# Down projection by half-size matrix products: first-half products of all pairs ahead, next operands prepared in mid-chunk

## The chip, the cores and the metric

One core of one Trainium2 chip. The time is the device time of one execution in microseconds (us), lower is better; the kernel before has a median of 1379.69 us over 3 runs.

## The reference, cut to what matters

One layer of a decoder trunk over 1024 tokens with 1024 channels, all in f32. The part that matters here is the channel mixer and what follows it:

```python
h = rmsnorm(x, g_ffn[i])
u = jnp.einsum("bsd,df->bsf", h, w_up[i])                 # 1024 -> 2 x 2816
f_gate = causal_dwconv(u[..., :D_FF], conv_f_w[i]) + conv_f_b[i]
f = jax.nn.gelu(f_gate, approximate=True) * u[..., D_FF:]
x = x + jnp.einsum("bsf,fd->bsd", f, w_down[i])           # 2816 -> 1024, the stage that is changed
pg = jax.nn.sigmoid(jnp.einsum("bsd,de->bse", rmsnorm(x, g_ple[i]), w_ple_gate[i]))
x = x + pg * jnp.einsum("bsk,kd->bsd", p[i], w_ple[i])
```

## The kernel before

**Layout.** Channels lie on the 128 partitions, tokens on the free axis. A tile ("slot") is 128 x 1024 f32; 54 slots (`NBIG`) hold everything, weights in flight too. `H0` and `H1` are the first and second 512 tokens. A matmul multiplies a 128 x 128 weight block by 128 x 512 activations into one of 8 PSUM banks. To keep f32 accuracy every operand is split: `halve` writes hi (a rounding copy on ACT, L132) and lo (a subtraction on DVE, L133), and a block product is three matmuls, hi*hi, hi*lo and lo*hi (L629).

**Seven products instead of eight.** A 2 x 2 block product (two output row tiles, two token halves, two input row tiles) is made by a Strassen-like scheme, class `Pair`: product 1 and 2 use the plain halves, products 3 to 7 use sums of weight blocks and (3 excepted, on the activation side) sums of activation halves. Products 1 and 2 accumulate in bank `a`, a copy of product 1 goes to bank `b` (ACT, L639) and products 6, 7 and 4 are added to it; products 5 and 3 accumulate in bank `c`. In between, `b` is copied to `e` after 6 and after 7 (ACT, L646 and L652). After 2, `use11` takes `a`; when 5 and 7 are both made, `sum(22)` reads `c` and `e`; after 4, `use21` takes `b`; after 3, `sum(12)` reads `c` and `e`. Product 3 is accumulated in the bank that `sum(22)` has to have read. In the up projection that read is L665.

**The down projection.** `f`, the 22 row tiles of the up projection's result, is stored to DRAM (`f_d`) and read back in three chunks of 4, 4 and 3 rows (`DROWS`); row i of a chunk is a pair of tiles, `f_d[k]` and `f_d[11 + k]`. For each chunk four output pairs (tiles j and j + 4) make their seven products, 3n matmuls each for n rows. The results of the first two chunks go through `dn` tiles to `x1_d` in DRAM by an accumulating DMA on POOL (L1152, class `DnStore`); the last chunk adds them to `x1`, loaded back, in SBUF (class `DnLast`, L1173) and makes the scaled halves `xp` and the square sums for the last stage.

**Operands of a chunk.** Class `Rows`: `load` fetches the two tiles of a row (512 KB each); `plain` splits the first halves for products 1 and 2 (`f_q`); `sums` makes four half-width sums (L586 to L589, `t13` and `t24`), splits both sums tiles (`fs`, `ft`) and the half of product 3 (`f_q`). `prepare` calls them by how many products are left before the chunk: loads at 14 (chunk 0: at 6 and 3), plain at 5 (chunk 0: 5 and 3), sums of row 0 at 2, of row 1 at 1, of rows 2 and 3 at 0.

**Weights.** Class `Loader` issues weight loads on SP in the order of their use, each a fixed number of matmuls ahead (`AHEAD`: r, for products 1 and 2, 110; q, for product 4, 100; s, the sums for products 3, 5, 6 and 7, 150) and as far as slots are free. The sums of an s weight are made by four accumulating DMAs on POOL, in a chain (L243, L244). A weight is split 40 matmuls ahead of its use.

**Order.** PE and SP run in the order of the program text. ACT, DVE and POOL are ordered by a scheduler that takes what it thinks is ready, earliest in the text first, with its own costs; on the chip each engine then works strictly in that order. `block_order(4, 2)` gives the order of products in a chunk; m is the product's number and p the pair:

```python
# block_order(4, 2): (p, m)
# (0,1) (1,1) (0,2) (1,2) (0,6) (0,5) (0,7) (0,4) (1,6) (0,3) (1,5) (1,7)
# (2,1) (1,4) (2,6) (2,2) (1,3) (2,5) (2,7)
# (3,1) (2,4) (3,6) (3,2) (2,3) (3,7) (3,5) (3,4) (3,3)
```

The up projection has 22 pairs in the same scheme with 12 matmuls a product and ends with (21,7), (21,5), (21,4), (21,3). After each of its last products `f_rows.prepare(0, left)` is called.

Of the kernel before, what the change touches and what calls it, by code (L numbers as in the profile page):

```python
# [8 lines left out]
F32R = mybir.dt.float32r  # L9
# [20 lines left out]
HB = 512  # L30
# [44 lines left out]
def trunk_kernel(ctx, tc, xT, pT, par, w_in, w_a, w_b, w_o, w_up, w_dn, w_ple, w_pg, outT):  # L75
# [54 lines left out]
    def halve(hi, lo, src):  # L130

        nc.scalar.copy(hi, src)  # L132
        nc.vector.tensor_sub(lo, src, f32(hi))  # L133
# [191 lines left out]

    def in_tiles(kind, i):
# [25 lines left out]
    dn_order = block_order(KD // 2, 2)  # L352
    for ci, (k0, n) in enumerate(DROWS):
        ld.add_pairs(("dn", ci), [(w_dn[j], w_dn[KD // 2 + j]) for j in range(KD // 2)], dn_order, k0, KH + k0, n)
# [4 lines left out]
    with tc.manual_schedule(engines={PE, SP}):  # L359
# [241 lines left out]
        def half_split(src, name):  # L601

            t = slot(name, F32R)
            halve(t[:, :HB], t[:, HB:], src)
            return t[:, :HB], t[:, HB:]
# [482 lines left out]
        class Rows:  # L1088


            def __init__(self):
                self.rows = [[{} for _ in range(n)] for _, n in DROWS]
                self.raw = {}

            def load(self, ci, i):
                k = DROWS[ci][0] + i
                self.raw[ci, i] = load(f_d[k], "f"), load(f_d[KH + k], "f")

            def plain(self, ci, i):
                a, b = self.raw[ci, i]  # L1100
                r = self.rows[ci][i]
                r[1], r[2] = half_split(a[:, H0], "f_q"), half_split(b[:, H0], "f_q")

            def sums(self, ci, i):
                a, b = self.raw[ci, i]
                r = self.rows[ci][i]
                r.update(sum_halves(*right_sums(a[:, H0], a[:, H1], b[:, H0], b[:, H1]), "f"))
                r[3] = half_split(b[:, H1], "f_q")

            def prepare(self, ci, left):  # L1110

                n = DROWS[ci][1]
                if left == (6 if ci == 0 else 14):
                    for i in range(2 if ci == 0 else n):
                        self.load(ci, i)
                if left == 5:
                    for i in range(2 if ci == 0 else n):
                        self.plain(ci, i)
                if left == 3 and ci == 0:
                    for i in range(2, n):  # L1120
                        self.load(ci, i)
                        self.plain(ci, i)
                if left == 2:
                    self.sums(ci, 0)
                if left == 1:
                    self.sums(ci, 1)
                if left == 0:
                    for i in range(2, n):
# [313 lines left out]
```

## Time and profile before

| | us |
|---|---|
| median of 3 runs (1376.6 to 1381.29) | 1379.69 |
| the profiled execution, as timed | 1382.37 |
| its span, first to last instruction | 1380.6 |
| TensorE busy in the span | 1306.8 |
| mean granted TensorE clock, share of full | 0.972 |

Times within the trace are microseconds from the start of the span. A row of a timeline is an instruction (or several alike, x2) with its start, its duration and, in brackets, how long its engine had been idle and what ended that. Matmuls are pipelined, so one has a duration of 0.39 us although the next begins 0.23 us later; pace is read from starts. A view by stretch gives each engine's busy time within a stretch, the mean granted TensorE clock, the mean busy share of the 16 DMA engines and what they moved. SPq and POOLq are the queues on which DMAs are issued.

### The profile page before, as it was taken

Reading aid. Unit: us, or ns where it says so; the run is one execution under the profiler, and the core shown is the slowest. Engines: PE = TensorE matmul, PEld = TensorE weight load, DVE = VectorE, ACT = ScalarE, POOL = GpSimd, SP = SyncE. Lnnn points to the kernel's source line nnn. Section 1 sums busy time; section 2 is a strip of 40 time slices with the busy share of each in tenths; the row PEclk is TensorE's granted clock in tenths of the full one; section 3 lists DMA queues with packets and bytes.
Section 4 is the critical chain, followed back from the end, with each engine's and each line's share of the span. In section 5 each row is a group of like instructions: output and inputs, shape, how many; then the busy total and the mean of one; then the engine's idle time right before and its main releaser. Section 6 shows DMA issues by size and latency. Waiting matters only on the chain.

```text
span 1380.6 us, 15699 instructions
## 1 busy us (share of the span) xinstructions
PE 1306.8 (95%) x5798; PEld 1081.9 (78%) x5798; DVE 976.6 (71%) x1134; ACT 590.3 (43%) x814; POOL 247.1 (18%) x319
## 2 busy tenths in 40 slices
PE   9989999999999999899999999999976979989996
PEld 7768888788887788778888888888864867867996
DVE  7969999999448766486665566665676292588787
ACT  7443233233444334354344433444344262456554
POOL 1331221122100001122221222212112222320011
PEclk9989999999999999999999999999998999999998
DMA  9645696578676303597666776667666998994222
GB/s 339 183 119 125 179 237 159 142 200 212 196 272 233 122 24 130 163 205 189 177 167 175 198 186 172 174 168 192 187 181 162 272 222 204 211 234 153 76 91 73
DMA packets 102765, 245.25 MB, mean 178 GB/s; under 512 B 11680, under 2 KB 21664, under 8 KB 102688
## 3 DMA queue, kind: packets, MB, share of 16 engines
q1 hardware_dynamic: 61632, 148.81, 32.6%
q0 software_dynamic: 41056, 95.44, 32.1%
q8 instruction: 45, 0.74, 0.2%
q14 instruction: 32, 0.26, 0.1%
HBM read 173.42 MB, written 45.09 MB: 158 GB/s over the span
## 4 chain that ended last, share of the span: by engine, by line
PE 71%; DVE 14%; issue 8%; DMA 3%; ACT 2%; POOL 1%; SPq 0%; DVEq 0%; ACTq 0%; POOLq 0%
PE ps L629 50%; PE ps L155 14%; DVE acc L712 2%; PE ps L969 2%; PE ps L968 2%; PE ps L970 2%; DMA x_d<-dn 2%; DVE w_s_lo L133 1%; POOL s L244 1%; DMA f<-f_d 1%; DVE w_r_lo L133 1%; DVE x_raw L477 1%; DVE ft_lo L133 1%; DVE sc_cv L712 1%; DVE t L588 1%
## 5 line engine op out<-in xcount | busy, mean ns | idle before, releaser
L712 DVE SCALAR_TENSOR_TENSOR acc<-a,prm,acc 128x1023 f32<-128x1023 f32 (+14 forms) x120 | 151.8, 1265 | 1.7
L133 DVE TENSOR_TENSOR w_s_lo<-s,w_s_hi 128x1024 fp32r<-128x1024 f32 (+1 forms) x100 | 119.6, 1198 | 35.7 <-ACT w_s_hi L132 35.7
L244 POOL DMA_DIRECT2D s<-s x100 | 85.6, 856 | 298.2 <-DMA s<-s 126.0
L652 ACT COPY u<-ps 128x512 f32<-128x512 f32 x50 | 29.3, 586 | 202.3 <-PE ps L629 202.3
L132 ACT CAST w_s_hi<-s 128x1024 fp32r<-128x1024 f32 (+1 forms) x100 | 102.9, 1031 | 2.6 <-issue 1.7
L712 DVE SCALAR_TENSOR_TENSOR fg<-u_t,neg_f,fg 128x1023 f32<-128x1023 f32 (+1 forms) x44 | 56.5, 1283 | 28.3 <-ACT fg L706 27.6
L133 DVE TENSOR_TENSOR w_r_lo<-raw_r,w_r_hi 128x1024 fp32r<-128x1024 f32 (+1 forms) x50 | 59.8, 1197 | 17.2 <-ACT w_r_hi L132 17.2
L646 ACT COPY u<-ps 128x512 f32<-128x512 f32 x50 | 29.3, 586 | 92.4 <-PE ps L629 92.4
L629 PE MATMUL ps<-xgs_hi,w_s_lo 128*128 128x512 f32 x176 | 68.6, 390 | 0.0
L629 PE MATMUL ps<-xgs_lo,w_s_hi 128*128 128x512 f32 x176 | 68.5, 389 | 0.0
L629 PE MATMUL ps<-xgs_hi,w_s_hi 128*128 128x512 f32 x176 | 68.5, 389 | 0.0
L629 PE MATMUL ps<-xgp_hi,w_r_lo 128*128 128x512 f32 x176 | 68.5, 389 | 0.0
L629 PE MATMUL ps<-xgp_lo,w_r_hi 128*128 128x512 f32 x176 | 68.5, 389 | 0.0
L629 PE MATMUL ps<-xgp_hi,w_r_hi 128*128 128x512 f32 x176 | 68.5, 389 | 0.0
L639 ACT COPY ps<-ps 128x512 f32<-128x512 f32 x50 | 28.5, 571 | 87.6 <-PE ps L629 87.6
L1075 DVE TENSOR_TENSOR u_t<-ps,rstd 128x512 f32<-128x512 f32 x22 | 15.2, 691 | 69.7 <-PE ps L629 69.7
L155 PE MATMUL ps<-xp_hi,whi 128*128 128x448 f32 (+2 forms) x192 | 62.0, 323 | 1.9 <-DVE x L1201 1.9
L629 PE MATMUL ps<-xgq,w_s_hi 128*128 128x512 f32 x176 | 55.8, 399 | 7.2 <-DVE u_t L665 7.2
L155 PE MATMUL ps<-xp_lo,whi 128*128 128x448 f32 (+2 forms) x192 | 61.9, 323 | 0.0
L155 PE MATMUL ps<-xp_hi,wlo 128*128 128x448 f32 (+2 forms) x192 | 61.9, 323 | 0.0
L629 PE MATMUL ps<-xgt_hi,w_q 128*128 128x512 f32 x176 | 57.9, 390 | 0.7 <-ACT u L652 0.7
L629 PE MATMUL ps<-hss_hi,w_s_hi 128*128 128x512 f32 x128 | 50.9, 398 | 4.5 <-ACT w_s_hi L132 4.5
(297 smaller groups left out, 3718.7 us busy)
## 6 DMA issues: line engine op xcount, KB each, us to landing
s<-s POOLq DMA_DIRECT2D x92, 256.0 KB, 4.1
raw_r<-w_up SPq DMA_DIRECT2D x22, 512.0 KB, 4.7
s<-w_up SPq DMA_DIRECT2D x44, 256.0 KB, 3.0
s<-w_up SPq DMA_DIRECT2D x22, 512.0 KB, 5.8
s<-w_up POOLq DMA_DIRECT2D x44, 256.0 KB, 6.0
f_d<-v_t POOLq DMA_DIRECT2D x22, 512.0 KB, 5.9
f<-f_d SPq DMA_DIRECT2D x22, 512.0 KB, 9.8
s<-w_in SPq DMA_DIRECT2D x32, 256.0 KB, 3.2
```

The lines of the kernel that those rows point to most:

```text
L132: nc.scalar.copy(hi, src)
L133: nc.vector.tensor_sub(lo, src, f32(hi))
L155: nc.tensor.matmul(ps[:, :step], wt[:, b], xt[:, t : t + step], start=f, stop=l)
L244: nc.gpsimd.dma_start(dst, src, accum_op=ALU.add)
L629: nc.tensor.matmul(ps, wt[:, b], xt, start=f, stop=l, skip_group_check=True)
L639: nc.scalar.copy(self.b, self.a)
L646: nc.scalar.copy(self.e[:, H0], self.b)
L652: nc.scalar.copy(self.e[:, H1], self.b)
L712: nc.vector.scalar_tensor_tensor(dst[:, s:], src[:, : T - s], w(k), dst[:, s:], ALU.mult, ALU.add)
L968: nc.tensor.matmul(ps, whi[:, b], hi, start=first and k == ks[0], stop=False)
L969: nc.tensor.matmul(ps, whi[:, b], lo, start=False, stop=False)
L970: nc.tensor.matmul(ps, wlo[:, b], hi, start=False, stop=last and k == ks[-1])
```

## The change

The order of products within a chunk becomes a function of the chunk, `dn_order(ci)`. Every chunk begins with products 1 and 2 of all four pairs, then come the others, pair by pair interleaved:

```python
# after (0..3, 1) and (0..3, 2):
# (0,6) (0,5) (0,7) (1,6) (0,4) (1,5) (0,3) (1,7) (2,6) (1,4) (2,5) (1,3) (2,7)
# chunks 0, 1: (3,6) (2,4) (2,3) (3,7) (3,5) (3,4) (3,3)
# chunk 2:     (3,6) (2,4) (3,7) (2,3) (3,4) (3,5) (3,3)
```

`Rows` is rewritten. A row's first halves (H0 of both tiles) go into one slot by two DMAs of 256 KB, its second halves into another; the four sums are made in place in these two slots, and the three splits are steps of their own. The table `STEPS` gives for each step and row at which product, counted from the chunk's start, it stands in the text (negative: before), first for chunk 0, then for the others. The first ACT copy of a row's plain split and the first subtraction of its sums are pinned behind everything traced before them on their engine. `DnStore` adds each half tile to `x1_d` as soon as it is there (32 adds of 256 KB instead of 16 of 512 KB), two halves sharing a slot. `DnLast` loads tile j with product 1 and tile j + 4 with product 6.

```diff
@@ -127,9 +127,11 @@
     def f32(ap):
         return ap.bitcast(F32)
-    def halve(hi, lo, src):
-        nc.scalar.copy(hi, src)
+    def halve(hi, lo, src, pinned=False):
+        ins = nc.scalar.copy(hi, src)
+        if pinned:
+            tc.keep_in_program_order(ins)
         nc.vector.tensor_sub(lo, src, f32(hi))
     def split(src, name, scale=None):
@@ -323,6 +325,20 @@
             order += [(p, 5), (p, 7)] if p < n - 1 else [(p, 7), (p, 5)]
         return order + [(n - 1, 4), (n - 1, 3)]
+    def dn_order(ci):
+        if ci == 0:
+            order = [(p, m) for m in (1, 2) for p in range(4)]
+        else:
+            order = [(0, 1), (1, 1), (0, 2), (2, 1), (1, 2), (3, 1), (2, 2), (3, 2)]
+        order += [(0, 6), (0, 5), (0, 7)]
+        for p in (1, 2):
+            order += [(p, 6), (p - 1, 4), (p, 5), (p - 1, 3), (p, 7)]
+        if ci < len(DROWS) - 1:
+            return order + [(3, 6), (2, 4), (2, 3), (3, 7), (3, 5), (3, 4), (3, 3)]
+        return order + [(3, 6), (2, 4), (3, 7), (2, 3), (3, 4), (3, 5), (3, 3)]
     def in_tiles(kind, i):
         return {
@@ -349,9 +365,9 @@
     for j in O_ORDER:
         ld.add(w_o[j], 8)
     ld.add_pairs("up", [(w_up[KF + j], w_up[j]) for j in range(KF)], up_order)
-    dn_order = block_order(KD // 2, 2)
     for ci, (k0, n) in enumerate(DROWS):
-        ld.add_pairs(("dn", ci), [(w_dn[j], w_dn[KD // 2 + j]) for j in range(KD // 2)], dn_order, k0, KH + k0, n)
+        pairs = [(w_dn[j], w_dn[KD // 2 + j]) for j in range(KD // 2)]
+        ld.add_pairs(("dn", ci), pairs, dn_order(ci), k0, KH + k0, n)
     for j in range(KD):
         ld.add(w_pg[j], 8, kind="late")
     ld.sort()
@@ -598,10 +614,10 @@
             out[6], out[4] = (hi[:, H0], lo[:, H0]), (hi[:, H1], lo[:, H1])
             return out
-        def half_split(src, name):
+        def half_split(src, name, pinned=False):
             t = slot(name, F32R)
-            halve(t[:, :HB], t[:, HB:], src)
+            halve(t[:, :HB], t[:, HB:], src, pinned)
             return t[:, :HB], t[:, HB:]
         class Pair:
@@ -1088,45 +1104,72 @@
         class Rows:
+            STEPS = {
+                "load0": ((-8, -8, -8, -8), (-20, -19, -18, -17)),
+                "plain": ((-3, -3, -2, -2), (-12, -11, -10, -9)),
+                "load1": ((-2, -2, -2, -2), (-14, -13, -12, -11)),
+                "sums13": ((1, 1, 2, 2), (-8, -7, -6, -5)),
+                "sums24": ((2, 2, 3, 3), (-4, -3, -2, -1)),
+                "split23": ((3, 3, 4, 4), (0, 1, 2, 3)),
+                "split14": ((5, 5, 6, 6), (1, 2, 3, 4)),
+            }
             def __init__(self):
                 self.rows = [[{} for _ in range(n)] for _, n in DROWS]
-                self.raw = {}
-            def load(self, ci, i):
+                self.s0, self.s1 = {}, {}
+            def load(self, ci, i, c):
                 k = DROWS[ci][0] + i
-                self.raw[ci, i] = load(f_d[k], "f"), load(f_d[KH + k], "f")
+                t = slot("f")
+                nc.sync.dma_start(t[:, H0], f_d[k][:, c])
+                nc.sync.dma_start(t[:, H1], f_d[KH + k][:, c])
+                return t
+            def load0(self, ci, i):
+                self.s0[ci, i] = self.load(ci, i, H0)
+            def load1(self, ci, i):
+                self.s1[ci, i] = self.load(ci, i, H1)
             def plain(self, ci, i):
-                a, b = self.raw[ci, i]
+                t, r = self.s0[ci, i], self.rows[ci][i]
+                r[1], r[2] = half_split(t[:, H0], "f_1", True), half_split(t[:, H1], "f_2")
+            def sums13(self, ci, i):
+                t, v = self.s0[ci, i], self.s1[ci, i]
+                tc.keep_in_program_order(nc.vector.tensor_sub(t[:, H0], t[:, H0], v[:, H0]))
+                nc.vector.tensor_sub(v[:, H0], v[:, H1], v[:, H0])
+            def sums24(self, ci, i):
+                t, v = self.s0[ci, i], self.s1[ci, i]
+                self.rows[ci][i][3] = half_split(v[:, H1], "f_3")
+                nc.vector.scalar_tensor_tensor(v[:, H1], t[:, H0], -1.0, v[:, H1], ALU.mult, ALU.subtract)
+                nc.vector.scalar_tensor_tensor(t[:, H1], v[:, H1], -1.0, t[:, H1], ALU.mult, ALU.subtract)
+            def halves(self, ci, i, t, ma, mb):
+                hi, lo = split(t, "f_s")
                 r = self.rows[ci][i]
-                r[1], r[2] = half_split(a[:, H0], "f_q"), half_split(b[:, H0], "f_q")
-            def sums(self, ci, i):
-                a, b = self.raw[ci, i]
-                r = self.rows[ci][i]
-                r.update(sum_halves(*right_sums(a[:, H0], a[:, H1], b[:, H0], b[:, H1]), "f"))
-                r[3] = half_split(b[:, H1], "f_q")
-            def prepare(self, ci, left):
-                n = DROWS[ci][1]
-                if left == (6 if ci == 0 else 14):
-                    for i in range(2 if ci == 0 else n):
-                        self.load(ci, i)
-                if left == 5:
-                    for i in range(2 if ci == 0 else n):
-                        self.plain(ci, i)
-                if left == 3 and ci == 0:
-                    for i in range(2, n):
-                        self.load(ci, i)
-                        self.plain(ci, i)
-                if left == 2:
-                    self.sums(ci, 0)
-                if left == 1:
-                    self.sums(ci, 1)
-                if left == 0:
-                    for i in range(2, n):
-                        self.sums(ci, i)
+                r[ma], r[mb] = (hi[:, H0], lo[:, H0]), (hi[:, H1], lo[:, H1])
+            def split23(self, ci, i):
+                self.halves(ci, i, self.s1[ci, i], 7, 6)
+            def split14(self, ci, i):
+                self.halves(ci, i, self.s0[ci, i], 5, 4)
+            def prepare(self, ci, t):
+                if ci < len(DROWS):
+                    for step, at in self.STEPS.items():
+                        for i in range(DROWS[ci][1]):
+                            if at[min(ci, 1)][i] == t:
+                                getattr(self, step)(ci, i)
         f_rows = Rows()
         live = {}
@@ -1138,34 +1181,44 @@
             live[p].step(m)
             left = len(up_order) - 1 - n
-            f_rows.prepare(0, left)
+            f_rows.prepare(0, -left)
         rows = live = None
         class DnStore:
+            part = None
             def __init__(self, j):
-                self.j, self.o, self.n = j, (slot("dn"), slot("dn")), [0, 0]
-            def ready(self, i):
-                self.n[i] += 1
-                if self.n[i] == 2:
-                    nc.gpsimd.dma_start(x1_d[self.j + 4 * i], self.o[i], accum_op=ALU.add)
+                self.j = j
+            def out(self):
+                t = DnStore.part
+                DnStore.part = slot("dn") if t is None else None
+                return DnStore.part[:, H0] if t is None else t[:, H1]
+            def add(self, i, c, o):
+                nc.gpsimd.dma_start(x1_d[self.j + 4 * i][:, c], o, accum_op=ALU.add)
             def use11(self, ps):
-                nc.scalar.copy(self.o[0][:, H0], ps)
-                self.ready(0)
+                o = self.out()
+                nc.scalar.copy(o, ps)
+                self.add(0, H0, o)
             def use21(self, ps):
-                nc.scalar.activation(self.o[1][:, H0], ps, AF.Copy, scale=-1.0)
-                self.ready(1)
+                o = self.out()
+                nc.scalar.activation(o, ps, AF.Copy, scale=-1.0)
+                self.add(1, H0, o)
             def sum12(self, c, e):
-                nc.vector.tensor_add(self.o[0][:, H1], c, e)
-                self.ready(0)
+                o = self.out()
+                nc.vector.tensor_add(o, c, e)
+                self.add(0, H1, o)
             def sum22(self, c, e):
-                nc.vector.scalar_tensor_tensor(self.o[1][:, H1], c, -1.0, e, ALU.mult, ALU.subtract)
-                self.ready(1)
+                o = self.out()
+                nc.vector.scalar_tensor_tensor(o, c, -1.0, e, ALU.mult, ALU.subtract)
+                self.add(1, H1, o)
         x1, xg2 = [None] * KD, [None] * KD
         ssq = Ssq()
@@ -1173,9 +1226,11 @@
         class DnLast:
             def __init__(self, j):
                 self.j = j
-                for k in (j, j + 4):
-                    x1[k] = load(x1_d[k], "x2")
-                    xg2[k] = (slot("xp_hi", F32R), slot("xp_lo", F32R))
+                self.load(j)
+            def load(self, k):
+                x1[k] = load(x1_d[k], "x2")
+                xg2[k] = (slot("xp_hi", F32R), slot("xp_lo", F32R))
             def ready(self, k, c):
                 x = x1[k][:, c]
@@ -1210,12 +1265,15 @@
         for ci in range(len(DROWS)):
             last = ci == len(DROWS) - 1
             live = {}
-            for n, (p, m) in enumerate(dn_order):
+            order = dn_order(ci)
+            for n, (p, m) in enumerate(order):
                 if m == 1:
                     live[p] = Pair(f_rows.rows[ci], (DnLast if last else DnStore)(p))
+                if m == 6 and last:
+                    live[p].to.load(p + 4)
                 live[p].step(m)
-                if not last:
-                    f_rows.prepare(ci + 1, len(dn_order) - 1 - n)
+                f_rows.prepare(ci, n + 1)
+                f_rows.prepare(ci + 1, n + 1 - len(order))
         live = None
```

## Rows read from the trace of the kernel before

**Rows 1.** The page's busy time: engine, busy us, share of the span, instructions.

```profile
PE 1306.8 (95%) x5798; PEld 1081.9 (78%) x5798; DVE 976.6 (71%) x1134; ACT 590.3 (43%) x814; POOL 247.1 (18%) x319
```

**Rows 2.** Busy time by stretch: us, each engine (instructions), PE clock, DMA share, GB/s.

```profile
1011.48:1023.68 12.20, 5.03 (x14) 3.89 (x14) 8.06 (x12) 4.46 (x6) 1.71 (x2) 0.72 0.73 184
1023.68:1117.75 94.07, 80.42 (x338) 64.55 (x336) 52.85 (x65) 41.87 (x60) 19.45 (x23) 0.93 0.77 196
1117.75:1206.21 88.46, 79.61 (x337) 64.55 (x336) 47.02 (x59) 38.22 (x55) 20.08 (x25) 0.94 0.89 216
1206.21:1272.59 66.38, 60.26 (x253) 47.98 (x251) 57.98 (x83) 41.31 (x65) 9.29 (x11) 0.95 0.69 187
```

**Rows 3.** PE in time order: start, us, line, operation, [idle before, releaser].

```profile
1117.75 0.62 PE L629 MATMUL ps<-f_q,w_r_hi 128*128 128x512 f32 x2
...
1128.40 0.39 PE L629 MATMUL ps<-f_q,w_r_lo 128*128 128x512 f32 x1
1136.66 0.80 PE L629 MATMUL ps<-ft_hi,w_s_hi 128*128 128x512 f32 x1 [7.87 <-ACT w_s_hi L132]
```

**Rows 4.** PE's waits, 980 to 1290: total us, times, longest.

```profile
PE ps L629 <- ACT w_s_hi L132: 24.4, 3, 12.0
PE ps L629 <- DVE u_t L665: 7.2, 1, 7.2
PE ps L629 <- ACT u L652: 2.0, 3, 0.7
```

**Rows 5.** Busy time by stretch again, right after that gap.

```profile
1136.66:1148.96 12.30, 11.31 (x37) 8.31 (x37) 4.48 (x6) 4.55 (x8) 0.84 (x1) 0.76 0.60 167
```

**Rows 6.** DVE in time order, at the boundary of chunks 0 and 1.

```profile
1105.49 4.91 DVE L133 TENSOR_TENSOR f_q<-f,f_q 128x512 fp32r<-128x512 f32 x8 [6.51 <-ACT f_q L132]
...
1113.25 0.68 DVE L586 TENSOR_TENSOR t<-f 128x512 f32<-128x512 f32 x1
...
1135.17 1.23 DVE L133 TENSOR_TENSOR ft_lo<-t,ft_hi 128x1024 fp32r<-128x1024 f32 x1
1136.31 0.68 DVE L133 TENSOR_TENSOR f_q<-f,f_q 128x512 fp32r<-128x512 f32 x1
```

**Rows 7.** DVE, then ACT, in time order at the up projection's end.

```profile
995.36 0.69 DVE L1075 TENSOR_TENSOR u_t<-ps,rstd 128x512 f32<-128x512 f32 x1 [3.40 <-PE ps L629]
...
1013.50 0.69 DVE L133 TENSOR_TENSOR f_q<-f,f_q 128x512 fp32r<-128x512 f32 x1 [1.92 <-ACT f_q L132]
...
1018.08 0.68 DVE L665 TENSOR_TENSOR u_t<-ps,u 128x512 f32<-128x512 f32 x1
...
1001.07 1.06 ACT L1080 ACTIVATE fg<-fg 128x1024 f32<-128x1024 f32 x1 [2.32 <-DVE fg L712]
...
1015.34 0.62 ACT L132 CAST f_q<-f 128x512 fp32r<-128x512 f32 x1 [1.87 <-DMA f<-f_d]
```

**Rows 8.** DMA, 1000 to 1275: queues; then issues, KB each, us to landing.

```profile
q0 software_dynamic: 9216, 20.45, 41.8%
q1 hardware_dynamic: 15804, 35.32, 38.1%
...
f<-f_d SPq DMA_DIRECT2D x18, 512.0 KB, 10.4
x_d<-dn POOLq DMA_DIRECT2D x16, 512.0 KB, 8.5
s<-w_dn SPq DMA_DIRECT2D x28, 256.0 KB, 4.6
x<-x_d SPq DMA_DIRECT2D x8, 512.0 KB, 4.8
```

**Rows 9.** SP, then POOL, in time order: DMA issues of one weight sum.

```profile
1135.26 0.33 SPq L240 DMA_DIRECT2D s<-w_dn  x1
...
1152.90 0.88 POOL L1152 DMA_DIRECT2D x_d<-dn  x1 [11.42 <-ACT dn L1159]
...
1170.06 0.84 POOL L244 DMA_DIRECT2D s<-s  x1 [8.00 <-DMA s<-s]
```


## The prediction

> **What bounds the kernel now.** The page's busy table comes first: TensorE (PE) is busy 95% of the span [rows 1], so nothing elsewhere can shorten this kernel except by closing gaps of PE. The view of busy time by stretch shows where the gaps of this stage are. I cut it at the first matmul of each chunk. The last product of the up projection and the three chunks of the down projection take 12.20, 94.07, 88.46 and 66.38 us [rows 2]. What they would take without a gap follows from PE's order of time at the start of chunk 1: 48 matmuls of two half-token products per pair begin between 1117.75 and 1128.40, 47 steps, 0.2266 us each [rows 3]. A chunk of n rows has 28 products of 3n matmuls: 336, 336 and 252, or 76.1, 76.1 and 57.1 us; the last product of the up projection has 12, or 2.7 us. So the four stretches lose 9.5, 17.9, 12.3 and 9.3 us, **49.0 us together**.
>
> Who is waited for: PE's waits in this part name ACT w_s_hi (24.4 us, three times, up to 12.0), DVE u_t once (7.2) and ACT u three times (2.0) [rows 4]. After a long wait the loss goes on: behind the 7.87 us gap at 1136.66 [rows 3] the granted clock of the next 12.3 us is only 0.76 on the mean [rows 5]: PE starts at its 1.2 GHz level after idling and comes back to 2.4 GHz.
>
> Why ACT w_s_hi is late: it isn't the weight. DVE runs without a break from the eight f_q at 1105.49 to the last f_q at 1136.31 [rows 6], and w_s_hi sits on ACT in the same train of splits. In that train each of the four rows costs four half-width sums, two full splits and one half split, 5 x 0.60 + 2 x 1.14 = 5.3 us at the pitch at which they follow one another (eight in 4.91; from 1135.17 to 1136.31). It is asked for in the last products of a chunk, and only four products (10.9 us) can run before the first one that needs sums. The 7.2 us at the end of the up projection is the same thing with loads: ACT's f_q at 1015.34 waits for the load of f, DVE's f_q behind it, and DVE's L665, whose read frees the bank for the last up product, comes after them at 1018.08 [rows 7].
>
> **The change part by part.**
>
> Order of products. Eight products instead of four need only plain rows, so the first product with sums is due 8 x 2.72 = 21.8 us after a chunk's start instead of 10.9; in the third chunk 16.3 instead of 8.2. No matmul is added. The order also puts another pair's product between (0,7) and (0,4), so the three ACT u waits [rows 4] go: 2.0 us of the 49.0.
>
> Preparation of chunks 1 and 2. Sums start eight products ahead and splits end four behind the start: 12 products, 32.6 us, for a train of 4 x 5.3 = 21.2 us. The DVE ops are the same in number and form (in place changes no width). Over chunk 1 DVE is busy 47.0 of 88.5 us [rows 2]; squeezed into 76.1 that is 62%. The eight products ahead of the boundary hold, at pitch, sums and f_3 of four rows (12.0), four r splits (4.6), two to three other weight splits (2.9), four outputs (2.4): 21.9 against 21.8 us. That is full, but nothing there is due on the spot, and the last r split has nine microseconds. I take the gap of chunk 1 as gone, less 1 us (bounds 0 and 4).
>
> Chunk 0 and the end of the up projection. Plain rows need only the first halves, asked for before the last eight products; 8 x 256 KB are half of what the queue ahead of L665 needed before. So u_t's 7.2 us and its clock loss go: 9.5 us. The sums are pinned behind all DVE work traced before, so behind L1085 of the last pair. One pair earlier, L1075 at 995.36 leads to the end of L1080 at 1002.13 [rows 7], 6.8 us. With (21,4) ending at 1011.6, L1085 ends near 1019.7. Then four rows of five half-width ops and one split, 16.6 us, and one weight split, 1.2, end at 1037.5, or 1040 with two r splits among them. (0,6) is due at 1014.2 + 21.8 = 1036.0 and its fourth row 2 us later: 0 to 2 us late. Splits for (0,5) add 4.6: again 2. I give back 4 us (bounds 0 and 9: all six products' splits in one row).
>
> Chunk 2. DVE is busy 58.0 of 66.4 us there [rows 2]. Ten half-width ops (6.8) and three r splits of three quarters of the width (some 0.9 each) leave for chunk 1, two splits of row 0 come in (2.4): 50.9 in 57.1, 89% by durations. Two places tighten. (3,3) now follows (3,5) at once, and waits for L1206 and L1207 to read the bank: one or two ops of 0.69, about 1 us. And the x1 tile of pair 3 is loaded ahead of the sixth product, while the last add into it leaves only after chunk 1 ends; an add took 8.5 us and the load about half that [rows 8], so use11 of pair 3 (due at 16.3 us) waits some microseconds on DVE, with few splits behind it. I give back 3 us (bounds 1 and 8).
>
> Transfers. f is loaded by 44 DMAs of 256 KB instead of 22 of 512 KB, on SP; x1 gets 32 adds instead of 16, on POOL, at 0.88 us of POOL each [rows 9]: 14 us of POOL, which is busy 19.5 and 20.1 us in the first two chunks [rows 2], so it hides there. Bytes are unchanged. In 1000 to 1275 the two queues hold 41.8% and 38.1% of the engines' time, 220 us. The stage would last 226, so the cover is nearly gone. Price of the halves, from both sides. By bytes: a 256 KB load took 4.6 us where a 512 KB one took 10.4 [rows 8], so nothing is added. By packets: 2048 more on 9216 (22% of 115 us) and 2816 more on 15804 (18% of 105 us), +44 us of engine time. I take a value near the first, because that row is the same queue in the same stretch, and give back 2 us.
>
> One rule speaks against this part. The Trainium skill (Perfetto Trace Analysis, section DMA Optimizations) holds that batching from 2 KB to 4 KB can raise throughput a lot where DMA bounds, and that splitting pays where the engines are mostly idle; here they are not, and the change splits. The two load rows above do not bear the rule out at this size; what it would give is the second rival.
>
> **Sum** against the profiled execution (1382.4 us, span 1380.6): 49.0 - 4 - 1 - 3 - 2 = **39 us saved**, 1343.4. The median of the runs lies 2.7 us below that execution, so I forecast **1341 us**. By the bounds of chunk 0 to 2 (1 to 21 given back) this case alone spans 1332 to 1352.
>
> **Rivals.**
> 1. *A queue still blocks at the end of the up projection.* Only the first half split and the first sum of a row are pinned; the ACT copies of f_2 and f_3 can be ordered ahead of a load that lands later than the scheduler thinks, as f_q was [rows 7]. Then 9.5 us stay: 1351. Against it: the loads are asked for earlier.
> 2. *DMA takes PE's place as the bound.* For it: 220 us of engine time in a stage of 226. With the packet price it is 264, the stage gains 275 - 264 = 11 us: 1369. At half that price 242, gain 33 less the 8 above: 1355. I put it at 1362. Against: the load rows, and between 1000 and 1275 engines stood idle a fifth of the time [rows 8].
> 3. *Slower: s weights come late behind the adds on POOL.* Each pair's sums of weights are a chain of four accumulating DMAs on POOL, which is in order, and adds wait there for products. At 1152.90 POOL had waited 11.42 us for dn, and the chain whose load SP issued at 1135.26 got its last DMA at 1170.06 [rows 9], to land some 5 us on if it takes as long as a 256 KB load [rows 8]: 40 us. Its lead is 150 matmuls, 34 us. With twice the adds, if every one of 11 chains took 40, PE would wait 6 us for each: 66 us against 39 gained, 1407. It turns to slower from 3.5 us of lateness a chain. Against: an add now leaves as soon as its half is there, so waits on POOL get shorter, and the slow chain above delayed no product.
>
> **How the numbers follow.** Forecast 0.62, rival 1 0.12, rival 2 0.18, rival 3 0.08. Comparisons of this kernel can tell about 0.3% (4 us) from no change. Slower by more: 0.08 (rival 3). Within: 0.04, where rival 2's packet price meets the 8 us given back elsewhere (1377). Faster: 0.88. The range runs from 1328 (nearly all of the 49, less 3 us for the spread of the runs before) to 1368, which takes in the forecast, rival 1 and about half of rival 2, so some 0.83.
>
> **What would show it.** Right: no PE wait over 2 us between the last up product and the first gate product; chunks of 76 to 81, 76 to 80 and 58 to 65 us; DVE's train of splits broken up over 12 products; granted clock near 1.00 there; DMA share above 0.9. Wrong: a PE wait on w_s_hi or w_s_lo in mid-chunk with DMA s<-s behind it (rival 3, or rival 2 if the share stands at 1); DVE L665 still behind an f split that waits for a load (rival 1); (0,6) or (0,5) of chunk 0 waiting more than 9 us. The forecast fails if the scheduler's order of ACT and DVE differs from the order of the text by more than the leads used here.

## The result, and the profile after

The changed kernel takes **1356.2 us** (median of four runs, 1354.6 to 1358.2) against 1378.1 us of the kernel before in the same comparison (1376.4 to 1381.3): ratio 0.9839, interval 0.9813 to 0.9865, **22 us faster**. The forecast was 1341 and 39 us. The sign and the range held; 17 of the 39 us did not come. The profiled execution took 1358.2 us with a span of 1356.4.

Busy time by stretch, the changed kernel, cut as in [rows 2]: the last up product, then chunks 0, 1 and 2.

```profile
1010.55:1013.41 2.86, 2.86 (x12) 2.37 (x13) 2.86 (x5) 0.17 (x1) 0.00 (x0) 1.00 1.06 385
1013.41:1101.36 87.95, 79.82 (x337) 63.91 (x336) 64.91 (x85) 45.34 (x65) 25.17 (x30) 0.96 0.97 236
1101.36:1178.08 76.72, 76.53 (x338) 62.96 (x337) 46.27 (x58) 37.09 (x54) 27.73 (x32) 1.00 0.98 232
1178.08:1249.34 71.26, 62.38 (x253) 49.89 (x251) 51.81 (x74) 39.43 (x62) 14.81 (x17) 0.93 0.74 192
```

Against 2.7, 76.1, 76.1 and 57.1 us without a gap (336 matmuls at 0.2266 us [rows 3]), the losses are 0.1, 11.8, 0.6 and 14.1 us where they were 9.5, 17.9, 12.3 and 9.3: 26.6 of 49.0 are left, so 22.4 are won in these stretches. They are cut from the two profiled executions, whose spans differ by 24.2 us (1380.6 and 1356.4); the other 1.9 us lie before and behind them, and the medians differ by 22. The end of the up projection and chunk 1 are clean. **Chunk 0 kept two thirds of its loss, and chunk 2 has become worse.**

PE's waits from 980 to 1290 in the changed kernel (total us, times, longest), to be held against [rows 4]:

```profile
PE ps L645 <- ACT ps L655: 4.8, 2, 4.7
PE ps L645 <- ACT u L662: 3.4, 2, 2.2
PE ps L645 <- ACT w_s_hi L132: 2.8, 1, 2.8
PE ps L645 <- DVE w_s_lo L135: 2.5, 1, 2.5
PE ps L645 <- ACT w_r_hi L132: 1.6, 1, 1.6
PE ps L645 <- DVE w_r_lo L135: 1.2, 2, 0.6
...
PE ps L645 <- DVE x L1262: 0.8, 1, 0.8
```

The 24.4 us on w_s_hi and the 7.2 us on u_t are gone. What is new is L655, ScalarE's copy of product 1's result: 4.7 us, in chunk 2.

The two engines behind these waits. ScalarE (ACT) in time order, changed kernel, at the start of chunk 0 and in chunk 2:

```profile
1008.53 2.18 ACT L132 CAST f<-f 128x512 fp32r<-128x512 f32 x4
1016.33 0.57 ACT L655 COPY ps<-ps 128x512 f32<-128x512 f32 x1 [5.61 <-PE ps L645]
1016.81 1.05 ACT L132 CAST w_r_hi<-raw_r 128x1024 fp32r<-128x1024 f32 x1
...
1022.25 1.06 ACT L1096 ACTIVATE fg<-fg 128x1024 f32<-128x1024 f32 x1
...
1194.34 0.63 ACT L434 ACTIVATE ssq<-x 128x512 f32<-128x512 f32 x1 [6.70 <-DMA x_d<-dn]
...
1196.54 0.58 ACT L655 COPY ps<-ps 128x512 f32<-128x512 f32 x1
```

In chunk 0, ACT idles 5.61 us in front of a copy that waits for product (0,1) of the new chunk, while the weight splits w_r_hi and the last up pair's gate (L722, then L1096) stand behind it in ACT's order. In chunk 2 it idles 6.70 us for a tile: all tiles of this size come from one pool, and the one that L434 is to write is still being read by an add into x1. The copy of (3,1) stands behind, and PE waits 4.7 us for it.

VectorE (DVE) in time order, changed kernel: the train that ends before product (0,6), and chunk 2.

```profile
1023.34 1.23 DVE L1101 TENSOR_TENSOR v_t<-v_t,fg 128x1024 f32<-128x1024 f32 x1 [0.57 <-ACT fg L1096]
...
1025.62 0.69 DVE L1146 TENSOR_TENSOR f<-f 128x512 f32<-128x512 f32 x1
...
1038.80 5.76 DVE L135 TENSOR_TENSOR f_s_lo<-f,f_s_hi 128x1024 fp32r<-128x1024 f32 x5
1044.47 1.22 DVE L135 TENSOR_TENSOR w_s_lo<-s,w_s_hi 128x1024 fp32r<-128x1024 f32 x1
...
1205.42 0.69 DVE L1245 TENSOR_TENSOR x<-ps,x 128x512 f32<-128x512 f32 x1 [5.53 <-DMA x<-x_d]
```

And why the add and the load of chunk 2 are late, POOL and then SP in time order:

```profile
1188.53 1.20 POOL L1201 DMA_DIRECT2D x_d<-dn  x1
1193.31 0.85 POOL L246 DMA_DIRECT2D s<-s  x1 [3.58 <-DMA s<-s]
1193.84 2.09 POOL L1201 DMA_DIRECT2D x_d<-dn  x2
...
1183.82 18.30 SPq L872 DMA_DIRECT2D x<-x_d  x2
```

Chunk 1 ended at 1178.08; its last adds leave at 1188.53 and 1193.84, because they stand on POOL behind the accumulating transfers of weight sums: the one at 1193.31 had waited 3.58 us for its own predecessor, and two adds leave right behind it. SP is in order too: its row joins two loads, by the order of the text those of the x1 tiles 2 and 3, and the second is held 17.5 us until the adds into tile 3 have landed, so that it is issued near 1202. DVE waits for it 5.53 us at 1205.42, and PE, behind DVE and ACT, 2.2 us.

The transfers, 1000 to 1250, changed kernel (queues; then issues, KB each, us to landing), against [rows 8]:

```profile
q0 software_dynamic: 11808, 20.98, 48.8%
q1 hardware_dynamic: 18178, 34.91, 41.6%
...
f<-f_d SPq DMA_DIRECT2D x36, 256.0 KB, 6.8
x_d<-dn POOLq DMA_DIRECT2D x32, 256.0 KB, 7.2
s<-w_dn SPq DMA_DIRECT2D x28, 256.0 KB, 7.5
```

90.4% of 250 us are 226 us of engine time, against 220 of before, for nearly the same bytes (55.9 and 55.8 MB) in 28 and 15% more packets.

### The profile page after: what moved, and what is told of

It reads as the page before. It is cut to its first block, busy times and chain, and to the rows that moved or that the text cites. A ratio compares the mean times of both kernels' runs of the same rounds, so it can differ in the third digit from the quotient of the medians.

```text
span 1356.4 us, 15768 instructions
## 1 busy us (share of the span) xinstructions
PE 1302.8 (96%) x5798; PEld 1079.4 (80%) x5798; DVE 976.8 (72%) x1134; ACT 588.4 (43%) x814; POOL 261.8 (19%) x335
## 3 DMA queue, kind: packets, MB, share of 16 engines
q1 hardware_dynamic: 64800, 148.81, 33.2%
## 4 chain that ended last, share of the span: by engine, by line
PE 68%; DVE 14%; issue 8%; DMA 6%; ACT 2%; POOL 1%; SPq 0%; DVEq 0%; POOLq 0%; ACTq 0%
PE ps L645 48%; PE ps L157 13%; DVE acc L728 3%; PE ps L984 2%; PE ps L986 2%; PE ps L985 2%; DMA s<-w_dn 2%; DMA s<-w_in 2%; DVE w_s_lo L135 1%; DMA s<-s 1%; DVE ssq L442 1%; POOL s L246 1%; DVE h_lo L498 1%; DMA x_d<-dn 1%; POOL x_d L1201 1%
## 5 line engine op out<-in xcount | busy, mean ns | idle before, releaser
L655 ACT COPY ps<-ps 128x512 f32<-128x512 f32 x50 | 28.6, 572 | 82.1 <-PE ps L645 82.1
L645 PE MATMUL ps<-f,w_r_hi 128*128 128x512 f32 x176 | 56.0, 401 | 6.5 <-ACT ps L655 4.8
L645 PE MATMUL ps<-f_s_hi,w_s_hi 128*128 128x512 f32 x132 | 53.5, 405 | 6.3 <-ACT u L662 3.4
```

The source lines that it names most:

```text
L645: nc.tensor.matmul(ps, wt[:, b], xt, start=f, stop=l, skip_group_check=True)
L655: nc.scalar.copy(self.b, self.a)
```

## The experiments

All times are medians, each beside the kernel before on the same chip; a difference is the ratio's distance from 1 times 1380 us. Theory after the traces: chunk 0 loses to ACT's copy and to DVE's train, chunk 2 to chunk 1's last adds. Rivals: the gain is all in one part of the change; the halved transfers cost or earn something; the order inside the train matters and not its length.

**Order alone** (kernel before, new order of products and the load of tile j + 4 at product 6, old preparation):

```diff
+    def dn_order(ci):          # as in the change
...
-            for n, (p, m) in enumerate(dn_order):
+            for n, (p, m) in enumerate(order):
```

> The kernel before with the new order of products alone (and DnLast's load of tile j + 4 moved to product 6); loads, plain splits, sums and whole-tile adds stay as they were. If the order carries the gain (eight products of cover instead of four): the waits on w_s_hi at the three chunk starts (12.0, 7.9, 4.6 us) shrink by up to 10.9, 10.9 and 8.2 us to 1, 0 and 0 with their clock loss, the 7.2 us wait on u_t stays: 1346 to 1354 us. If the order is worth little without early sums: 1365 or more.

Measured 1381.4 us, ratio 1.0008 (0.9993 to 1.0022): **nothing**. PE's waits of this kernel, and ACT in time order in chunk 1:

```profile
PE ps L642 <- ACT w_r_hi L132: 26.0, 5, 11.3
```

```profile
1113.60 1.05 ACT L132 CAST w_r_hi<-raw_r 128x1024 fp32r<-128x1024 f32 x1
...
1131.18 0.61 ACT L132 CAST f_q<-f 128x512 fp32r<-128x512 f32 x1
1131.70 1.99 ACT L132 CAST w_r_hi<-raw_r 128x1024 fp32r<-128x1024 f32 x2
```

The wait on w_s_hi (24.4 [rows 4]) is now one on w_r_hi. Eight plain products need the weights of four pairs, and their splits stand behind the old train of sums, 18 us long, at the chunk's start. Products that are not due yet are no slack when what they need is in the same queue.

**Preparation alone** (changed kernel, halved transfers included, old order):

```diff
     def dn_order(ci):
+        return block_order(KD // 2, 2)
...
-                "split14": ((5, 5, 6, 6), (1, 2, 3, 4)),
+                "split14": ((4, 4, 5, 5), (1, 2, 3, 4)),
```

> The changed kernel with the old order of products (two pairs ahead, sums due after four products); preparation in mid-chunk, in-place sums and halved transfers stay; the splits of chunk 0 stand one product earlier because the old order asks for them. If preparation alone suffices: chunk 1 and 2 start without a gap as in the changed kernel and the 7.2 us on u_t are gone, but chunk 0's train of sums, which cannot start before the last gelu, misses its products by about 15 to 25 us: 1360 to 1372 us. If the order is not needed: 1356 as the changed kernel.

Measured 1374.4 us, 0.9962 (0.9949 to 0.9975): 5 us gained, and 2 us above the expected band of 1360 to 1372. Its PE waits:

```profile
PE ps L634 <- ACT w_r_hi L132: 10.7, 3, 5.3
PE ps L634 <- DVE f_s_lo L135: 7.2, 6, 4.7
```

Here the sums are due after 10.9 us and come later. 0 and 5 us apart, 22 together: neither part gives its gain without the other.

**No late adds** (changed kernel without chunk 1's four adds into the x1 tiles 3 and 7):

```diff
             def add(self, i, c, o):
+                if (DnStore.ci, self.j) == (1, 3):
+                    return
```

> The changed kernel without the four adds into x1 of pair 3 of chunk 1 (that part of the result is left out of the sum). If chunk 2's 14 us are lost because these adds leave POOL late behind sums of weights, and ACT's square waits for a slot that an add still reads while use11 of pair 3 waits for the load behind the last add: the waits of 4.7 and 2.2 us go with their clock loss, chunk 2 falls from 71.3 to 58 to 63 us and the time by 8 to 13 us, to 1343 to 1348. If DVE or the DMA engines bind chunk 2: it stays above 67 us and the time above 1351.

Measured 1347.1 us, 0.9767 (0.9735 to 0.9798): 32 us below before, **10 below the changed kernel**, as expected. Chunk 2:

```profile
1178.79:1241.10 62.31, 59.01 (x253) 48.01 (x251) 51.95 (x73) 39.61 (x62) 10.42 (x13) 0.97 0.71 194
```

71.3 us became 62.3, and both the 4.7 and the 2.2 us wait went: the held tile and the late load have one cause.

**Pinned copy** (changed kernel; ACT's copy of product 1 keeps its place in the written order in chunk 0):

```diff
-                    nc.scalar.copy(self.b, self.a)
+                    cp = nc.scalar.copy(self.b, self.a)
+                    if self.pin:               # chunk 0 only
+                        tc.keep_in_program_order(cp)
```

> The changed kernel with ACT's copy of product 1 (line 655) pinned, in chunk 0 alone, behind all ACT work that stands before it in the text. If chunk 0's 11.8 us come from that copy standing ahead of the weight splits and of the last pair's first convolution step on ACT while it waits for PE: the waits on w_r go (1.6, 0.5, 0.6 us), the last gelu ends some 3 us earlier, so do the sums, and the waits of 2.8 and 2.5 us shrink to under 3 together; chunk 0 falls from 88.0 to 79 to 83 us, the time to 1347 to 1351. If loads or DVE's own length set them: no change beyond 2 us.

Measured 1350.4 us, 0.9791 (0.9769 to 0.9813): 6 to 7 us below the changed kernel, in the expected band. Chunk 0 took 84.6 us, not 79 to 83: the w_r waits went (0.6 left), but (0,6) still waits 2.4 and 2.4 us for its split weight sum. So the copy was 3.4 us of chunk 0's 11.8; a further 2.4 us came in chunk 2 (71.3 to 68.8), which I had not expected: the last adds of chunk 1 left 9.4 and 13.7 us after its end instead of 10.5 and 15.8, and the wait on L655 there fell from 4.7 to 2.5 us.

**Whole adds** (changed kernel; results again in whole tiles, 16 adds of 512 KB):

```diff
...
+                if self.n[i] == 2:
+                    nc.gpsimd.dma_start(x1_d[self.j + 4 * i], self.o[i], accum_op=ALU.add)
```

> The changed kernel with one thing undone: the results of chunks 0 and 1 are again kept in two tiles of 128x1024 per pair and each is added to x1 by one transfer of 512 KB, 16 in all, where the changed kernel issues 32 of 256 KB. Theory A (the halves cost what their bytes cost: in the changed kernel the transfer time of the same stretch rose by some 6 us of 220 us of engine time, and the chunks are not held by it): chunks 0 and 1 stay as in the changed kernel within 2 us each. What it then does is one thing in chunk 2: an add leaves only when the second half of its tile is ready, so the last adds into the x1 tiles 3 and 7 land no earlier; time 1355 to 1361. Theory B (small transfers cost by the packet, as the prediction's upper bound for the transfers had it): chunks 0 and 1 win 2 us or more each and the time is 1350 or less.

Measured 1361.7 us, 0.9867 (0.9854 to 0.9881): 4 us slower than the changed kernel by the ratios, whose intervals just overlap, just above A's band, and opposite to B. But A's "chunk 1 within 2 us" missed: it took 81.4 us, while chunks 0 and 2 took 87.9 and 71.3 as in the changed kernel. Chunk 1's stretch, then ACT and PE in time order in it:

```profile
1101.82:1183.23 81.41, 78.03 (x337) 64.11 (x336) 47.42 (x58) 37.89 (x54) 22.20 (x27) 0.98 0.95 231
```

```profile
1108.27 1.04 ACT L132 CAST w_r_hi<-raw_r 128x1024 fp32r<-128x1024 f32 x1 [6.61 <-DMA x_d<-dn]
...
1110.80 1.12 PE L645 MATMUL ps<-f,w_r_hi 128*128 128x512 f32 x2 [3.38 <-ACT ps L655]
```

So adding in halves is no cost here, and more likely an earning of some 4 us: with whole adds ACT waits in chunk 1 for a tile that an add still reads, and PE behind it. In the changed kernel PE's waits in chunk 1 are 0.2 us together.

**Both repairs** (pinned copy; pair 3's chunk 1 results stay in SBUF and are added by DVE behind the load of the x1 tile):

```diff
             def add(self, i, c, o):
+                if self.kept():                # chunk 1, pair 3
+                    return
...
                 x1[k] = load(x1_d[k], "x2")
+                if k in DnStore.held:
+                    nc.vector.tensor_add(x1[k], x1[k], DnStore.held.pop(k))
...
```

> The changed kernel with two edits together: the copy of product 1 keeps its place in the written order in chunk 0 (worth 6 us alone), and chunk 1's results of pair 3 stay in two tiles in SBUF and are added by VectorE to the x1 tiles 3 and 7 behind their load, so that no add is left out and none of them passes through DRAM (leaving the four adds out was worth 9 us). Theory: the two places are independent, chunk 0 as with the pinned copy alone (84.6 us) and chunk 2 as with the adds left out (62.3 us) plus two VectorE adds of 128x1024, some 1.2 us each, of which at most one stands before a sum that PE waits for: 1341 to 1345. Rival: the late x1 tiles were only half of chunk 2's loss, and the weight sums' chain on POOL sets the rest, or the two edits share one gain (the 6 us pinned copy already shortened chunk 2 from 71.3 to 68.8 us): 1346 to 1349.

Measured **1341.7 us, 0.9721** (0.9707 to 0.9734), as the theory had it: 38 us below before, 16 below the changed kernel. Its three chunks:

```profile
1013.31:1097.88 84.57, 79.14 (x337) 64.01 (x336) 64.71 (x85) 44.51 (x64) 26.10 (x31) 0.96 0.98 246
1097.88:1174.04 76.16, 76.16 (x337) 63.08 (x336) 47.18 (x58) 38.21 (x55) 28.51 (x33) 1.00 1.02 242
1174.04:1234.25 60.21, 57.75 (x253) 46.97 (x251) 53.30 (x75) 38.53 (x61) 9.52 (x11) 1.00 0.73 198
```

**The last chunk's end** (both repairs, and the order of the other chunks' end):

```diff
-        return order + [(3, 6), (2, 4), (3, 7), (2, 3), (3, 4), (3, 5), (3, 3)]
+        return order + [(3, 6), (2, 4), (2, 3), (3, 7), (3, 5), (3, 4), (3, 3)]
```

> The two edits together, and the end of the last chunk's order put as in the other chunks: (3,6), (2,4), (2,3), (3,7), (3,5), (3,4), (3,3), where the changed kernel has (3,6), (2,4), (3,7), (2,3), (3,4), (3,5), (3,3). Theory: what PE waits for in the last pair's products is that a product follows its own predecessor at once: (3,7) two places behind (3,6) waited 1.25 to 2.8 us for the copy of (3,6)'s result, and (3,3) behind (3,5) 0.78 us. With one more product between, the first goes; (3,3) then stands behind (3,4), whose result it doesn't wait for in the same way. 2 to 4 us less than the two edits alone. Rival: the changed kernel's end makes the last x1 halves come sooner for the sums behind the chunk, so what the chunk wins is given back there as a wait of the next projection: within 1 us of the two edits alone, or up to 3 us slower.

Measured 1345.3 us, 0.9752 (0.9739 to 0.9765): 4 us slower than both repairs alone, so the rival's side, a little beyond its 3 us. PE in time order at the last product:

```profile
1233.45 0.73 PE L645 MATMUL ps<-f,w_s_hi 128*128 128x512 f32 x2 [3.19 <-DVE x L1277]
```

The 1.25 us wait of (3,7) went and (3,3)'s grew from 1.21 to 3.19 us: the price moved within the chunk, 60.2 to 61.8 us. That is all by which the two profiled executions differ (spans 1340.8 and 1342.4); the rest of the 4 us between the medians isn't placed.

**Later splits** (both repairs; chunk 0's splits for products 5 and 4 later):

```diff
-                "split14": ((5, 5, 6, 6), (1, 2, 3, 4)),
+                "split14": ((8, 8, 9, 9), (1, 2, 3, 4)),
```

> The two edits together, and in chunk 0 the splits of the token sums for products 5 and 4 (step split14) at steps 8, 8, 9, 9 of the chunk instead of 5, 5, 6, 6, so that pair 0's weight sum is split ahead of them on ScalarE and VectorE (by two splits of 1.14 us on VectorE, by four of 0.95 us on ScalarE). Theory: what is left of chunk 0's loss (84.6 us against 76.1 us of matmuls) is product (0,6), which waited 2.4 us for the high and 2.4 us for the low part of that weight sum and then ran at a lowered clock, because VectorE works from 1013 to 1042 us without a gap and these parts stand near the end: chunk 0 79 to 82 us, the whole 2 to 5 us below the two edits alone. Rival: VectorE's work before product (0,6) is the bound and not its order; the wait moves to (0,6)'s own token splits or to (0,5), and the time stays within 1.5 us.

Measured 1341.3 us, 0.9719 (0.9706 to 0.9733): the same, the rival's value. Chunk 0 took 83.2 us instead of 84.6; the wait on w_s_hi went, w_s_lo is waited for 3.0 us and f_s_lo 1.2.

**No sums in chunk 0** (both repairs; without its token sums):

```diff
             def sums13(self, ci, i):
+                if ci == 0:
+                    return
...
                 self.rows[ci][i][3] = half_split(v[:, H1], "f_3")
+                if ci == 0:
+                    return
```

> The kernel with the two edits (pinned copy of product 1 in chunk 0, pair 3's results of chunk 1 kept in SBUF), and chunk 0's token sums left out: the 16 VectorE sums of 128x512 (four for each of four rows) aren't computed, and the operands of products 4 to 7 of chunk 0 are split from the unsummed tiles; that part of the computation is missing from the result. Nothing else moves. Theory: the length of VectorE's train is what is left of chunk 0's loss (84.5 us with the two edits, against 76.1 us of matmuls): it runs without a gap from 1006 us on, and 16 sums of 0.6 us, 9.7 us, stand ahead of pair 0's split weight sum, for which product (0,6) waits 4.8 us and after which TensorE runs at a lowered clock for a while. Without them the wait goes: chunk 0 76.5 to 78.5 us, the whole 6 to 8.5 us below the two edits' 1341.7, so 1333 to 1336. Rival: the weight sum arrives late (its chain of transfers on POOL's queue ends when it ends) or ScalarE is the bound; then product (0,6) waits nearly as before and the time stays above 1339.

Chunks 0 and 1:

```profile
1010.89:1088.47 77.58, 76.94 (x337) 62.83 (x336) 54.95 (x69) 44.85 (x64) 24.97 (x29) 1.00 1.04 258
1088.47:1167.13 78.66, 76.50 (x337) 62.98 (x336) 47.08 (x59) 37.95 (x55) 29.10 (x34) 1.00 1.01 242
```

Chunk 0 fell by 7.0 us to 77.6, inside the theory's band, with 9.8 us less of DVE and a granted clock of 1.00, and (0,6) waits for nothing: **the length of DVE's train is 7.0 of the 8.5 us that were left of chunk 0's loss.** The time fell less than expected, to 1339.1 us (1336.6 to 1343.9; 0.9713, 0.9692 to 0.9735), which is just on the rival's side and not clear of both repairs' 0.9721. So the reading rests on the chunks of the profiled execution, the fastest of the four: its chunk 1 lost 2.5 us to a 2.2 us wait on L655, and chunk 2 1.9 us, with a wait on u that grew from 1.3 to 2.0 us.

**One row first** (both repairs; on DVE pair 0's weight split behind one row's token split):

```diff
-                "split23": ((3, 3, 4, 4), (0, 1, 2, 3)),
-                "split14": ((5, 5, 6, 6), (1, 2, 3, 4)),
+                "split23": ((3, 7, 7, 7), (0, 1, 2, 3)),
+                "sums4": ((8, 8, 9, 9), (-4, -3, -2, -1)),
+                "split14": ((8, 8, 9, 9), (1, 2, 3, 4)),
...
```

> The kernel with the two edits, and chunk 0's preparation in the order in which product (0,6) eats it, nothing left out: the fourth sum of each row (needed by products 5 and 4 alone) and the splits of rows 1 to 3 for products 7 and 6 move to steps 7 to 9 of the chunk, so that on VectorE pair 0's split weight sum stands behind one row's token split and ahead of the others, some 4.6 us earlier in the train by the durations of the two edits' run (four splits of 1.14 us). Theory: it is the order of the train in front of product (0,6) that costs, since its first row needs one token split and one weight split, and rows follow each other by 2.7 us: both 2.4 us waits at its start go and the lowered clock behind them, chunk 0 77 to 80 us, the whole 1334 to 1338. Rival: only the amount of work counts (moving the other splits behind this product by two places each gave nothing: 1341.3 against 1341.7), so the wait is found again at the rows 1 to 3 or at product (0,5), and the time is 1340 or more.

Measured 1340.8 us, 0.9722 (0.9709 to 0.9735): the rival's value. Chunk 0's stretch, and DVE in time order:

```profile
1012.71:1095.95 83.24, 78.94 (x338) 62.29 (x336) 64.74 (x85) 44.45 (x64) 25.99 (x31) 1.00 1.01 250
```

```profile
1032.47 2.50 DVE L1159 SCALAR_TENSOR_TENSOR f<-f 128x512 f32<-128x512 f32 x4
1034.88 1.22 DVE L135 TENSOR_TENSOR w_s_lo<-s,w_s_hi 128x1024 fp32r<-128x1024 f32 x1
...
1043.97 2.36 DVE L135 TENSOR_TENSOR f_s_lo<-f,f_s_hi 128x1024 fp32r<-128x1024 f32 x2
```

w_s_lo starts at 1034.88 and (0,6) starts on time, but now it and (0,5) wait seven times for f_s_lo, 3.7 us together, and chunk 0 takes 83.2 us. DVE still ends its train at 1046 (1047 in both repairs). The fourth sums stand ahead of w_s_lo although they were written behind it, so this order is not quite the one intended; since the end of the train does not move, I read it with the run before as amount, not order.

## Why the prediction was right or wrong

- **What bounds the kernel** held: the four stretches' losses, 49.0 before and 26.6 after, make 22.4 of the 24.2 us between the profiled executions.
- **Its own signs** came in chunk 1 alone (76.7 us, granted clock 1.00, DMA share 0.98). Four PE waits were over 2 us (4.7, 2.8, 2.5 and 2.2), and chunks 0 and 2 lie above their bands of 76 to 81 and 58 to 65 us.
- **End of the up projection**: forecast all 9.5 us, measured 9.4. Rival 1 did not come there. Its cause, the scheduler ordering an ACT copy ahead of ready work, did come one step later: L655 in chunk 0.
- **Chunk 1**: give-back 1, measured 0.6. The count of 21.9 us of DVE work in 21.8 us, nothing of it due at once, was good enough.
- **Chunk 0**: give-back 4 (bounds 0 to 9), measured 11.8. Two steps were mis-sized. The gate's end was put at 1019.7 by shifting the pair before; it came at 1024.6. L655, which held ACT 5.6 us, is 2.2 us of that, since with the copy pinned the gate ended at 1022.4, and it is 3.4 us of chunk 0. The rest of the delay stays with the pin: DVE does splits for chunk 0 ahead of the gate's steps (1.89 us from 1011.50 on) and between them (2.35 us from 1018.88 on, both repairs), which the shift did not count. The train was put at 16.6 plus one weight split, 17.8 us; it took 20.1 us (1025.62 to 1045.7), since two of the splits for (0,5) stand ahead of the weight's, and I let those cost only after (0,6); moved behind, they gave 1.4 us of chunk 0. What remains with the copy pinned, 8.5 us, is 5.4 us of listed waits and 3 us beside them (last section), with a granted clock of 0.96 over the chunk; the give-back had no term for that. The last sentence of the prediction named the condition, an order of ACT and DVE other than the text's.
- **Chunk 2**: give-back 3 (bounds 1 to 8), measured 14.1. (3,3) behind (3,5) waited 0.8 us, as said. The x1 tile of pair 3 was seen, but timed from a free queue: an 8.5 us add and a load of about half that after chunk 1's end, some 13 us. DVE could go on with it 27.3 us after (1178.08 to 1205.42), because I moved the adds past POOL's issue time (0.88 us each) and not past what POOL waits for. The pool's tile held by the same adds, 6.7 us on ACT, was in no step. No late adds: 9.0 us of the 14.1 go at once.
- **Transfers**: give-back 2, between 0 by bytes and 44 by packets. Engine time of the stage rose by 6 us, and chunk 1 ran within 0.6 us of its matmuls at a DMA share of 0.98, so rival 2 is out. For the adds the term's sign was wrong as far as the ratios can tell: with them halved the kernel is some 4 us faster. The halved loads were not undone in a run of their own. The batching rule of the Trainium skill (Perfetto Trace Analysis, section DMA Optimizations), which the prediction weighed, is for kernels that DMA bounds. The engine time of POOL's queue, 449 us with halved adds against 442 with whole ones, lies in its direction, though hardly clear of the spread (last section), and did not decide the time here: the larger add was the slower kernel. The same section says that splitting may let some parts start sooner; in line with that, under whole adds ACT waited 6.61 us for a tile that an add still read.
- **Rival 3** did not come: PE's w_s waits are chunk 0's train. But its queue decided chunk 2 the other way round: the adds were late behind the weights, not the weights behind the adds.
- The chances (0.88 for faster) held by what chunk 1 and the up projection gave. That the range held is in part luck: the three chunks gave back 26.5 us, more than the 21 of their upper bounds together, and the time lies in the part of the range that was there for rivals 1 and 2, which did not come. (The span of 1332 to 1352 by those bounds leaves out the 2 us of the transfers; with them it is 1334 to 1354.) With the two places repaired, the time is the 1341 us that was forecast; that is an agreement of sums, since chunk 0 still loses 8.5 us there, twice its term, and chunk 1 next to nothing.

## What to carry to other kernels

A new order of work may pay only with the preparation moved to match, and the reverse (here 0 and 5 us alone, 22 together): do not drop either after a run of it alone, and do not add their gains. When a transfer is moved past a queue that is in order, time it from what that queue waits for, not from its issue cost, and ask which tiles it holds until it lands. Pin, or at least look up, the place of any copy that waits for the next stage's first result, since everything ready behind it on its engine waits too.

## What the runs showed of the hardware

- Halving transfers from 512 to 256 KB left their engine time near that of their bytes. POOL's queue over the whole execution, whole adds and then the changed kernel (packets, MB, share):

```profile
q0 software_dynamic: 41056, 95.44, 32.5%
q0 software_dynamic: 43360, 95.44, 33.1%
```

Of 1360.2 and 1356.4 us these are 442 and 449 us, so 2304 packets more cost some 7 us at most: SP's queue, with the same halved loads in both, differs as much (148.81 MB in 443 and 450 us). Before, with whole loads, it took 450. Times to landing did not halve: 7.2 us instead of 8.5 for x1 adds, 6.8 instead of 10.4 for f loads. They are no price of the size alone, since in the same stretch weight loads of 256 KB, unchanged, landed after 7.5 us instead of 4.6 (DMA share 0.97 in chunk 0, 0.77 before).
- A wait costs more than the idle time listed for it. PE in time order, in the run One row first:

```profile
1040.13 0.40 PE L645 MATMUL ps<-f_s_hi,w_s_hi 128*128 128x512 f32 x1
1041.84 0.51 PE L645 MATMUL ps<-f_s_lo,w_s_hi 128*128 128x512 f32 x1 [1.30 <-DVE f_s_lo L135]
1042.18 0.40 PE L645 MATMUL ps<-f_s_hi,w_s_lo 128*128 128x512 f32 x1
```

A step is 0.23 us without a wait. Here the step into the wait is 1.71 us and the one behind it 0.34, so 1.6 us are lost for 1.30 listed: idle time is counted from the end of a matmul 0.4 us long, which the next would have overlapped. The seven waits on f_s_lo, 3.7 us listed, cost 5.6 us by starts, most of the 7.1 us that chunk 0 lost there at a granted clock of 1.00.
- Some waits lower the clock, and their length alone doesn't tell which. In both repairs PE waited 2.40 us, ran two matmuls and waited 2.44 us:

```profile
1042.42 0.79 PE L645 MATMUL ps<-f_s_hi,w_s_lo 128*128 128x512 f32 x1 [2.44 <-DVE w_s_lo L135]
1043.01 0.63 PE L645 MATMUL ps<-f_s_hi,w_s_hi 128*128 128x512 f32 x1
```

From 1038.76, behind the first wait, to 1045.50 the granted clock was 0.51, the lower of the two levels (1.2 GHz), and steps were 0.43 us; behind that it was 1.00. Under later splits a single wait of 3.03 us left it at 1.00 (1040.94 to 1044.00). What decides isn't settled by these runs.
